# A hybrid decoder layer on one core: its beginning rewritten, and its buffers laid out without gaps

## The chip, the cores and the metric

The kernel runs on one NeuronCore of one Trainium2 chip. The metric is device time in microseconds (us), as the median of several executions. One execution was also recorded by the hardware profiler; the profile and the trace quoted here come from that one. The engines are named as the profile names them: PE (TensorE, matrix products; PEld is its weight load), ACT (ScalarE), DVE (VectorE), POOL (GpSimd) and SP (SyncE, which here only issues transfers). A 128x512 tile means 128 partitions with 512 elements of four bytes each.

## The reference, cut to what matters

For 2048 tokens of width 1024, one layer in float32:

```python
mod = silu(c) @ w_ada + b_ada                       # one row of 3 x 1024
shift, scale, gate = split(mod, 3)
h = rmsnorm(x, g_norm) * (1 + scale) + shift        # rmsnorm over the 1024 columns
proj = h @ w_in                                     # 2832 columns, cut into gq gk gv ga gz sq sk sv sz
z = ga @ w_decay + b_decay
o_gla = rmsnorm_per_head(gla_chunked(gq, gk, gv, log_sigmoid(z) / 16)) * silu(gz)
q, k = rope(sq), rope(sk)
o_swa = sliding_window_sink_attention(q, k, sv, sinks) * silu(sz)
y = concat(o_gla, o_swa) @ w_out
out = rmsnorm(x + gate * y, g_final)
```

The gated linear attention (gla) has 4 heads, worked in two pairs; the sliding-window attention (swa) has 8 query heads on 2 key heads, in blocks of 128 tokens.

## The kernel before, in words

**Precision.** A float32 operand of the large products is split into a high part (rounded to the fast format, F32R) and a low part (what is left), and a product is three fast matmuls: high by high, high by low, low by high (`mm3`). Names ending in h and l are these parts: `hh`, `hl` for the normalised input h, `wh`, `wl` for weights.

**Stages.** Tokens are worked in four groups of 512 (u = 0 to 3). For each group, h lies transposed, with 8 tiles over the 1024 columns (k = 0 to 7, called the eight steps of k), and the projection is done in slots of 256 columns, named by what they give: qk0, gz0, gv0 (272 columns, with the decay inputs), qk1, gz1, gv1, kv, sz0, sq0, sq1, sz1. At the end 16 output tiles (`py`) follow, 128 tokens each.

**The beginning (u = 0).** `silu_rows` spreads silu(c) over all partitions: eight float32 products of s_c by an identity matrix, into two 128x512 PSUM tiles (`pb`). `norm0_start` loads the eight 128x512 tiles of the transposed x, squares each on ACT, and sums over the columns by eight float32 products with a matrix of ones (`ss`); 20 products without use (`warm`, `pw`) follow; two ACT steps make the reciprocal root `rstd`. For each step of k, `ada_load` brings 1 MB of w_ada, `ada_cols` multiplies it by the silu rows on DVE (four 128x512 pieces, whose sums are collected in `part` and added), and ACT makes the shift and the scale of that column tile; `norm0_k` multiplies x by rstd (POOL, or DVE for k = 0), applies scale and shift on ACT, copies the high part on ACT and subtracts for the low part on DVE. Beside it, three 128x256 weight tiles of the slots qk0, gz0 and sz0 are loaded and split (high on ACT, low on POOL). `proj_t_outer` then runs all three slots together, step of k by step of k, 18 matmuls of 512 columns each, into six PSUM tiles (`po`).

**Weights.** In group 0 each slot is loaded raw (`wr`), split, used, and its two parts are written to a buffer in HBM (`wc`); groups 1 to 3 fetch the parts from there (`fetch`). The SBUF tile of a slot is 128 x 8 x 272; a slot of 256 columns leaves 16 columns of each of the 8 rows empty. Two such tiles (one in use, one being filled) are there for each part, and three staging tiles (`st`) for raw weights.

**Keys.** `k_rows` (L993) transposes the rotated keys of a group into one PSUM tile (`pkr`, bank pqk), copies them from there four times on ACT into the key tiles `kst`, and subtracts four times on DVE, reading `pkr` again. The same bank serves the transposed queries (`pq`).

**What sets the order.** All operations are first recorded (`Order`, L85) with a duration from a small cost model. `issue` (L207) then plays them through that model, engine by engine: of the operations that are ready at an engine's next free time, the one with the lowest number goes first (the numbers are lowered by `lift` for urgent and raised by `LATER` for unhurried ones). The resulting sequence of each engine is emitted; on the chip each engine follows its sequence and waits for its operands by semaphores. All large transfers are issued by SP, in order, on one queue. Because every operation is emitted by one helper, most rows of the profile carry the same line, and tiles are told apart by name.

## Time and profile before

| what | value |
|---|---|
| median of 3 runs | 867.58 us (866.02 to 867.92) |
| the profiled execution's own time | 866.11 us |
| its span in the profile | 864.4 us |
| PE busy | 839.3 us, 97% of the span |
| DVE, ACT, POOL busy | 66%, 55%, 43% |
| transfers | 179.90 MB, mean 208 GB/s |

A timeline row reads: start in us, length in us, engine, line, operation, output <- inputs (partitions x elements), count; in square brackets the idle time of the engine just before, and what ended it. A row with x2 or more holds several instructions. A wait list reads: who waited <- for whom: total us, how often, longest. A row of windows reads: from:to, length, then busy us of PE, PEld, DVE, ACT and POOL with their instruction counts, the clock granted to PE (1.00 is full), the mean busy share of the 16 transfer engines and GB/s. PE's busy time includes the modelled end of each matmul, so the distance from one start to the next tells its rate.

### The profile page before, as it was taken

To read this page: it belongs to the slowest core of one execution; us is meant where nothing else is said; L and a number is where in the kernel's file an instruction comes from. 1 tells how busy PE (TensorE), PEld (TensorE's weight loads), DVE (VectorE), ACT (ScalarE), POOL (GpSimd) and SP (SyncE) were. 2 spreads that over 40 slices of the span, in tenths; PEclk is the share of its full clock that TensorE was granted. 3 is DMA by queue.
4 is the path that set the end of the run, shared out by engine and by line. 5 is a ranking of instruction groups with operands and counts; after the bars stand their busy time and mean duration, and the time that the engine had idled before them with its cause. 6 is when DMAs were issued, how large, how long until landed. Compare 5 with 4: busy or idle time off the path is not lost. (4 is left out here: it accounts for less than half of the span.)

```text
span 864.4 us, 14761 instructions
## 1 busy us (share of the span) xinstructions
PE 839.3 (97%) x5126; PEld 730.9 (85%) x5126; DVE 572.9 (66%) x1157; ACT 476.0 (55%) x1197; POOL 372.4 (43%) x437
## 2 busy tenths in 40 slices
...
DMA  8999996963443475755337746669585855444411
GB/s 295 364 364 337 346 311 218 330 222 120 165 165 117 143 229 191 248 172 182 116 124 243 236 155 201 243 214 327 166 288 187 257 171 180 147 139 148 145 70 49
DMA packets 153119, 179.90 MB, mean 208 GB/s; under 512 B 8739, under 2 KB 121430, under 8 KB 151894
## 3 DMA queue, kind: packets, MB, share of 16 engines
...
q10 hardware_dynamic: 864, 0.04, 0.1%
HBM read 134.78 MB, written 44.17 MB: 207 GB/s over the span
## 5 line engine op out<-in xcount | busy, mean ns | idle before, releaser
L420 PE MATMUL py<-woh,m 128*128 128x512 f32 (+2 forms) x528 | 160.6, 385 | 0.0
L420 PEld LDWEIGHTS py<-woh,m 128*128 128x128 f32 x528 | 98.5, 188 | 19.5 <-issue 0.2
L420 PE MATMUL py<-wol,m 128*128 128x512 f32 (+2 forms) x264 | 101.6, 385 | 0.0
L373 POOL TENSOR_TENSOR r<-r,gf 128x512 f32<-128x512 f32 x31 | 45.1, 1453 | 116.4 <-ACT xr L373 116.4
L373 ACT ACTIVATE ge<-ge 128x512 f32<-128x512 f32 x96 | 60.7, 632 | 32.6 <-DVE ge L373 28.7
L420 PE MATMUL pn<-wh_gv,hh 128*128 128x272 f32 (+1 forms) x256 | 73.3, 286 | 0.9 <-DVE rope L373 0.9
L420 PE MATMUL pn<-wl_gv,hh 128*128 128x272 f32 (+1 forms) x256 | 73.5, 287 | 0.0
L420 PE MATMUL pn<-wh_gv,hl 128*128 128x272 f32 (+1 forms) x256 | 73.4, 287 | 0.0
L420 PE MATMUL pn<-wh_sq,hh 128*128 128x256 f32 x256 | 72.5, 283 | 0.0
L420 PE MATMUL pn<-wl_sq,hh 128*128 128x256 f32 x256 | 72.2, 282 | 0.0
L420 PE MATMUL pn<-wh_sq,hl 128*128 128x256 f32 x256 | 72.1, 282 | 0.0
L373 DVE TENSOR_TENSOR r<-py,xr 128x512 f32<-128x512 f32 (+2 forms) x33 | 22.3, 675 | 58.0 <-PE py L420 55.2
L373 ACT ACTIVATE s<-s,nm 128x128 f32<-128x128 f32 x128 | 50.0, 392 | 17.5 <-DVE nm L373 17.3
L420 PEld LDWEIGHTS py<-wol,m 128*128 128x128 f32 x264 | 49.6, 188 | 9.8
L373 POOL TENSOR_TENSOR s<-s,den 128x512 f32<-128x512 f32 x32 | 35.8, 1120 | 50.2 <-DVE den L373 25.1
L373 POOL TENSOR_TENSOR xt<-xt,rstd 128x512 f32<-128x512 f32 x31 | 41.9, 1359 | 27.9 <-ACT rstd L373 16.4
L373 POOL TENSOR_TENSOR o<-o,zs 128x128 f32<-128x128 f32 x64 | 31.3, 509 | 46.3 <-DVE o L373 46.3
L420 PEld LDWEIGHTS pn<-wh_gv,hh 128*128 128x128 f32 x256 | 48.2, 188 | 1.6 <-PE pn L420 1.1
L420 PEld LDWEIGHTS pn<-wl_sq,hh 128*128 128x128 f32 x256 | 48.2, 188 | 0.9 <-issue 0.2
L420 PEld LDWEIGHTS pn<-wh_sq,hh 128*128 128x128 f32 x256 | 48.3, 188 | 0.8 <-issue 0.2
L420 PEld LDWEIGHTS pn<-wh_sq,hl 128*128 128x128 f32 x256 | 48.3, 189 | 0.7
L420 PEld LDWEIGHTS pn<-wl_gv,hh 128*128 128x128 f32 x256 | 48.2, 188 | 0.7
...
## 6 DMA issues: line engine op xcount, KB each, us to landing
...
```

What stands on the lines that cost most here:

```text
L373: return order.add(eng, lambda: real(*args, **kw), dur, ins, outs, lock=lock, nbytes=nbytes)
L420: return od.add("PE", lambda: T.matmul(o, l, r, start=start, stop=stop), dur, [l, r] + ([] if start else [o]), [bank if start and bank is ...
```

## The change

**The beginning.** c is loaded by ACT's queue, so SP starts with x. x comes in four transfers of 128x1024 (rows of 4 KB in memory) instead of eight of 128x512; two column tiles are squared (one on ACT, one on DVE), added on DVE, and summed by one product, so `ss` takes four products instead of eight. The silu rows use F32R parts of s_c and of the identity: 16 fast products into one 128x1024 PSUM tile in a pool of its own. `ada_cols` takes each 128x1024 row of w_ada in one DVE instruction that also gives its sum. The three first weight tiles come as one transfer of 128x768 per step of k, and are split in two pieces. h's high part is written by ACT directly from x (with scale and shift), without a copy; for odd k (`WITH_V`) DVE applies scale and rstd, and makes the low part with the shift. The last step of rstd is written to PSUM, from where DVE reads it for k = 0; ACT copies it to SBUF. For k = 0 the 512 tokens are worked in two halves. 13 products without use stand in place of 20. The table of angles (`rope_tables`) is recorded to start after the last low part of h. sz0 takes the third place in the weight buffer.

**Keys.** `k_rows` copies `pkr` once into an SBUF tile `kt` (in the one buffer `ge`, which the gates and `dgh` use too); ACT and POOL copy from there, and DVE subtracts from there.

**Layout.** A slot of 256 columns lies in its tile without gaps (`flat_w`), so that a whole part is one row of 8 KB. `mixd`, the buffer of the mixed heads, is ordered by token block; xT by token group.

**The planner.** An operation that its model takes to need the port shared by DVE and POOL is ready no earlier than that port's free time (`PATIENCE`), and the model moves transfers at 330 GB/s in its first 20 us. The PSUM tiles ppt and ppo move to a pool `att2` that is opened after the beginning.

Three places show what moves. First, DVE at its start (`sq` are squares of x, `s_c` the silu column, `b` a bias row, `rr` and `rn` the table of angles, `wa` a row of w_ada). Before:

```order
L373 TENSOR_SCALAR s_c<-s_c 128x8
L373 RECIPROCAL s_c<-s_c 128x8
L373 TENSOR_TENSOR s_c<-s_c,c_sb 128x8
L373 TENSOR_SCALAR b_125<-b_sb 128x8
L373 TENSOR_TENSOR b_125<-b_125,g_sb 128x8
L373 CAST pos_f<-pos_i 128x16
L373 TENSOR_TENSOR rr_240<-pos_f,fr 128x512
L373 TENSOR_SCALAR rn_239<-rr_240 128x512
L373 TENSOR_SCALAR rn_239<-rn_239 128x512
L373 SCALAR_TENSOR_TENSOR wa_153,ap_157<-wa_153,pb_104 128x512
```

The same place on DVE in the changed kernel, from its first row:

```order
L377 TENSOR_TENSOR sq_113<-xt_111 128x512
L377 TENSOR_SCALAR s_c<-s_c 128x8
L377 RECIPROCAL s_c<-s_c 128x8
L377 TENSOR_TENSOR s_c<-s_c,c_sb 128x8
L377 TENSOR_TENSOR sq_115<-xt_111 128x512
L377 CAST s_ch<-s_c 128x8
L377 TENSOR_TENSOR sq_112<-sq_112,sq_113 128x512
L377 TENSOR_TENSOR s_cl<-s_c,s_ch 128x8
L377 TENSOR_TENSOR sq_114<-sq_114,sq_115 128x512
L377 TENSOR_TENSOR sq_117<-xt_111 128x512
L377 TENSOR_SCALAR b_123<-b_sb 128x8
L377 TENSOR_TENSOR sq_116<-sq_116,sq_117 128x512
```

The table of angles has gone from here, and four squares and four additions (six of the eight are among these rows) have come in ahead of the first product with w_ada.

Second, SP behind the loads of the beginning (`wr` raw weights, `wc` the buffer of split parts). Before:

```order
L373 DMA wr_sz_205<-in_w_in 128x256
L373 DMA wc<-wh_gz_131 128x512
L373 DMA wc<-wh_gz_132 128x512
L373 DMA wc<-wh_gz_133 128x512
L373 DMA wc<-wl_gz_135 128x512
L373 DMA wc<-wh_qk_129 128x8x256
L373 DMA wc<-wl_qk_130 128x8x256
L373 DMA wr_gv_214<-in_w_in 128x544
```

In the changed kernel:

```order
L377 DMA wr_first_180<-in_w_in 128x768
L377 DMA wr_gv_185<-in_w_in 128x544
L377 DMA wr_gv_186<-in_w_in 128x544
L377 DMA wr_gv_187<-in_w_in 128x544
L377 DMA wc<-wh_first 128x2048
L377 DMA wr_gv_188<-in_w_in 128x544
L377 DMA wc<-wl_first 128x2048
```

The last raw piece of gv0 now has one write of 1 MB between it and the others instead of six writes.

Third, PE at the start of slot sq0 (`pn` products of a slot, `pk`, `pc`, `po` pieces of gla; the digit behind hh or hl is k). Before:

```order
L420 MATMUL pn_321<-wh_sq_300,hh_5_193 128x256
L420 MATMUL pn_321<-wl_sq_301,hh_5_193 128x256
L420 MATMUL pn_321<-wh_sq_300,hl_5_194 128x256
L420 MATMUL pn_321<-wh_sq_300,hh_6_200 128x256
L420 MATMUL pn_321<-wl_sq_301,hh_6_200 128x256
L420 MATMUL po_279<-sT,v 128x128 x4
L420 MATMUL po_278<-qk_229,R_272 128x128
L420 MATMUL po_279<-qk_229,R_272 128x128
```

In the changed kernel:

```order
L424 MATMUL pn_303<-wh_sq_278,hh_0_153 128x256
L424 MATMUL pn_303<-wl_sq_279,hh_0_153 128x256
L424 MATMUL pn_303<-wh_sq_278,hl_0_154 128x256
L424 MATMUL pn_303<-wh_sq_278,hh_1_157 128x256
L424 MATMUL pn_303<-wl_sq_279,hh_1_157 128x256
L424 MATMUL pn_303<-wh_sq_278,hl_1_158 128x256
L424 MATMUL pn_303<-wh_sq_278,hh_2_161 128x256
L424 MATMUL pn_303<-wl_sq_279,hh_2_161 128x256
L424 MATMUL pn_303<-wh_sq_278,hl_2_162 128x256
L424 MATMUL pn_303<-wh_sq_278,hh_3_165 128x256
L424 MATMUL pn_303<-wl_sq_279,hh_3_165 128x256
L424 MATMUL pn_300<-wh_sq_278,hh_6_177 128x256 x2
```

Before, the first product with k = 6 stood directly behind those with k = 5. Now the two token blocks of `pn_300` stop at k = 5, the next block `pn_303` takes eleven products with k = 0 to 3, and only then does k = 6 follow; the pieces of gla `pk`, `pc`, `pu` and the first `po`, which before stood among the products of slot kv, have also come in behind the first product of sq0.

```diff
-WARM = (20, 20)
+WARM = 13
+WITH_V = (1, 3, 5, 7)
...
+PATIENCE = 0.0
...
+            if need[x[2]][2][0].lock:
+                t = max(t, self.port - PATIENCE)
...
-            self.wire = max(self.wire, t + 0.9) + o.bytes / 370e3
+            self.wire = max(self.wire, t + 0.9) + o.bytes / (330e3 if t < 20 else 370e3)
...
-    mixd = dram.tile([P, 8, S], F32, name="mixd")
+    mixd = dram.tile([P, S // P, 8, P], F32, name="mixd")
...
+        i.deps.add(ready[0])
...
+    rows = Pool("rows", 1, PSUM, into=ctx2)
...
-        rows = []
-        for i in range(2):
-            pb = att.tile([P, NB], F32, name=f"pb{i}", tag="ppt" if i == 0 else "ppo")
-            for k in range(4):
-                j = 4 * i + k
-                mmul(pb[:, k * P:(k + 1) * P], s_c[:, j:j + 1].broadcast_to([P, P]), ident, True, True)
-            rows.append(pb)
-        return rows
+        pb = rows.tile([P, D], F32, name="pb")
+        for j in range(KT):
+            with od.together():
+                for i in range(2):
+                    mmul(pb[:, j * P:(j + 1) * P], s_p[i][:, j:j + 1].broadcast_to([P, P]), ident_r,
+                         i == 0, i == 1)
+        return pb
...
-        part = begin.tile([P, 2, 2], F32, name=f"ap{j}", tag="ap", bufs=3)
         for i in range(2):
-            for h in range(2):
-                w_ = wa[:, i, h * NB:(h + 1) * NB]
-                V.scalar_tensor_tensor(w_, w_, 1.0, srow[h], op0=ALU.mult, op1=ALU.mult,
-                                       accum_out=part[:, i, h:h + 1])
-        V.tensor_reduce(ada[:, j], part, AX.X, ALU.add)
+            V.scalar_tensor_tensor(wa[:, i], wa[:, i], 1.0, srow, op0=ALU.mult, op1=ALU.mult,
+                                   accum_out=ada[:, j, i:i + 1])
         A.activation(ashift[:, j:j + 1], ada[:, j, 0:1], AF.Identity, bias=b_sb[:, j, 0:1])
...
+            raws[k] = begin.tile([P, 3, n], F32, name=f"wr_first{k}", tag="st0", bufs=3)
+            SY.dma_start(raws[k].rearrange("p a b -> p (a b)"), src[:, k])
+
+        def part(k):
+            raw = raws.pop(k)
+            both = ([t[:, k] for t in t0], raw[:, 0]), ([t[k] for t in t1], raw[:, 1:3])
+            for d, r in both:
+                (G.tensor_copy if k == 0 else A.copy)(d[0], r)
+            for d, r in both:
+                G.tensor_tensor(d[1], r, f(d[0]), ALU.subtract)
...
+                for k in range(KT):
+                    ops.append(SY.dma_start(f(to[:, :, k]), f(t1[i][k])))
+            od.lift = 0
+            for x in ops:
+                x.deps.add(after)
...
+    def flat_w(t, n):
+        return t.rearrange("p k n -> p (k n)")[:, :t.shape[1] * n].rearrange("p (k n) -> p k n", n=n)
...
+        if copy is None:
+            A.activation(th, xt, AF.Identity, bias=ashift[:, j:j + 1], scale=amul[:, j:j + 1])
         A.activation(xt, xt, AF.Identity, bias=ashift[:, j:j + 1], scale=amul[:, j:j + 1])
-        copy(th, xt)
-        V.tensor_tensor(tl, xt, f(th), ALU.subtract)
+        if copy is not None:
+            copy(th, xt)
...
-            xt = begin.tile([P, NB], F32, name=f"xt0_{j}", tag="xt0", bufs=KT)
-            SY.dma_start(xt, xT[j * P:(j + 1) * P, 0:NB])
-            xt0.append(xt)
-            sq = begin.tile([P, NB], F32, name=f"sq{j}", tag="sq", bufs=3)
-            A.activation(sq, xt, AF.Square)
-            i = mmul(ps, ones, sq, j == 0, j == KT - 1)
-        warm(WARM[1], i)
+        xs = begin.tile([P, KT, NB], F32, name="xt0")
+        for j in range(0, KT, 2):
+            SY.dma_start(xs[:, j:j + 2], xT[:, 0, j:j + 2])
+        for j in range(0, KT, 2):
+            sq = [stp.tile([P, 2, MAXN], F32, name=f"sq{j}", tag="st").rearrange("p a b -> p (a b)")[:, :NB],
+                  stp.tile([P, NB], F32, name=f"sq{j + 1}", tag="xs", bufs=2)]
+            A.activation(sq[0], xs[:, j], AF.Square)
+            V.tensor_tensor(sq[1], xs[:, j + 1], xs[:, j + 1], ALU.mult)
+            V.tensor_tensor(sq[0], sq[0], sq[1], ALU.add)
+            i = mmul(ps, ones, sq[0], j == 0, j == KT - 2)
+            xt0.extend([xs[:, j], xs[:, j + 1]])
+        warm(WARM, i)
         r = begin.tile([P, NB], F32, name="rstd0")
         A.activation(r, ps, AF.Ln, bias=eps_c, scale=1.0 / D)
-        A.activation(r, r, AF.Exp, scale=-0.5)
-        rstd[0] = r
+        A.activation(ps, r, AF.Exp, scale=-0.5)
+        rstd[:] = r, ps
+
+    def norm0_scale(j):
+        if j == 0:
+            V.tensor_tensor(xt0[j], xt0[j], rstd[1], ALU.mult)
+            A.copy(rstd[0], rstd[1])
+        elif j not in WITH_V:
+            G.tensor_tensor(xt0[j], xt0[j], rstd[0], ALU.mult)
 
     def norm0_k(j):
-        xt = xt0[j]
-        (G if j else V).tensor_tensor(xt, xt, rstd[0], ALU.mult)
         hh[j] = hp.tile([P, NB], F32R, name=f"hh0_{j}", tag="hh")
         hl[j] = hp.tile([P, NB], F32R, name=f"hl0_{j}", tag="hl")
-        h_split(j, xt, hh[j], hl[j], A.copy)
+        if j in WITH_V:
+            x_ = xt0[j]
+            V.scalar_tensor_tensor(x_, x_, amul[:, j:j + 1], rstd[0], op0=ALU.mult, op1=ALU.mult)
+            A.activation(hh[j], x_, AF.Identity, bias=ashift[:, j:j + 1])
+            ready[0] = V.scalar_tensor_tensor(hl[j], x_, ashift[:, j:j + 1], f(hh[j]),
+                                              op0=ALU.add, op1=ALU.subtract)
+            return
+        for h in halves(j):
+            h_split(j, xt0[j][:, h], hh[j][:, h], hl[j][:, h], None)
+
+    def halves(j):
...
+            for h in halves(k):
+                for i, w in enumerate(ws):
+                    for ct in range(2):
+                        cs = slice(ct * P, (ct + 1) * P)
+                        p = ps[2 * i + ct]
+
+                        for n, (a, b) in enumerate(((w[0], hh), (w[1], hh), (w[0], hl))):
+                            mmul(p[:, h], a[k][:, cs], b[k][:, h], k == 0 and h.start == 0 and n == 0,
+                                 k == KT - 1 and n == 2, p)
...
+            SY.dma_start(mixd[:, u * TPU:(u + 1) * TPU, 2 * pair + h], rt.rearrange("p (a b) -> p a b", a=TPU))
...
+        kt = near.tile([P, NB], F32, name="kt", tag="ge", bufs=1)
+        A.copy(kt, pt)
         for kv in range(2):
             src = half[kv]
             kh, kl = [x[:, P:] for x in kst[kv]]
-            for h in (src, half[1 - kv]):
-                A.copy(kh[h], pt[src])
-        for kv in range(2):
-            src = half[kv]
-            kh, kl = [x[:, P:] for x in kst[kv]]
+            A.copy(kh[src], kt[src])
+            G.tensor_copy(kh[half[1 - kv]], kt[src])
             for h in half:
-                V.tensor_tensor(kl[h], pt[src], f(kh[src]), ALU.subtract)
+                V.tensor_tensor(kl[h], kt[src], f(kh[src]), ALU.subtract)
 
     def sink_sq(u, kv, qr_of):
...
     def first_k(k):
         ada_load(k)
-        for w in wk:
-            w[2](k)
+        w_load(k)
+        if k == 0:
+            w_part(k)
+            norm0_scale(k)
         ada_cols(k)
         norm0_k(k)
+        if k > 0:
+            w_part(k)
+        if k + 1 < KT:
+            norm0_scale(k + 1)
 
     ps = proj_t_outer(wk, first_k)
     V.tensor_copy(pf, pos_i)
     loader(0, 0)
-    od.lift = LATER
-    for w in wk:
-        w[3]()
-    od.lift = 0
+    w_keep(ready[0])
     ctx2.close()
     keep = Pool("keep", 1)
     tmp = Pool("tmp", 2)
```

115 lines of the change are left out of this document (65 added, 50 removed).

## The prediction

> **What bounds the kernel now.** I read the page first, then the chain of waits, then PE's own waits, and then the timelines of the places that the change touches. The page:
>
> ```profile
> span 864.4 us, 14761 instructions
> PE 839.3 (97%) x5126; PEld 730.9 (85%) x5126; DVE 572.9 (66%) x1157; ACT 476.0 (55%) x1197; POOL 372.4 (43%) x437
> ```
>
> PE is the bound: 97% busy, and the other engines have a third of the time free or more. The chain ends with one unbroken stretch of the output products, of which the change alters nothing:
>
> ```profile
> 706.72 151.03 PE py L420 x684
> ```
>
> So the change can gain only where PE stands still or runs slowly before 706 us. The list of PE's waits names where (us in all, times, longest):
>
> ```profile
> PE pb L420 <- DVE b L373: 3.6, 1, 3.6
> PE pq L425 <- DVE kst L373: 2.9, 3, 1.1
> PE po L420 <- ACT hh L373: 2.8, 1, 2.8
> PE ppo L420 <- POOL ph L373: 2.2, 2, 1.3
> ...
> PE pg L420 <- ACT ga L373: 0.2, 1, 0.2
> ```
>
> The first and third lie in the beginning, the second in the keys; all fifteen rows sum to 17.9 us. The timeline of the beginning shows the chain behind them:
>
> ```profile
> 1.25 5.21 SPq L373 DMA_DIRECT2D xt<-in_xT  x8
> 3.57 3.75 PE L420 MATMUL pb<-ident,s_c 128*128 128x128 f32 x16 [3.57 <-DVE b L373]
> 4.69 1.30 ACT L373 ACTIVATE sq<-xt 128x512 f32<-128x512 f32 x2 [1.91 <-DMA xt<-in_xT]
> 7.11 7.97 PE L420 MATMUL ss<-sq,ones_r 128*128 128x512 f32 x16
> 12.56 0.69 DVE L373 SCALAR_TENSOR_TENSOR wa<-wa,pb 128x512 f32<-128x512 f32 x1 [3.71 <-PE ss L420]
> 14.92 4.63 PE L420 MATMUL pw<-ident,ones_r 128*128 128x128 f32 x40
> 15.18 0.69 ACT L373 ACTIVATE rstd<-ss,eps_c 128x512 f32<-128x512 f32 x1
> 16.90 0.62 ACT L373 ACTIVATE rstd<-rstd 128x512 f32<-128x512 f32 x1
> 17.60 1.60 POOL L373 TENSOR_TENSOR xt<-xt,rstd 128x512 f32<-128x512 f32 x1 [0.41 <-ACT rstd L373]
> 17.99 1.75 DVE L373 TENSOR_TENSOR xt<-xt,rstd 128x512 f32<-128x512 f32 x1
> 19.84 0.41 ACT L373 CAST wh_qk<-wr_qk 128x256 fp32r<-128x256 f32 x1 [2.04 <-DMA wr_qk<-in_w_in]
> 20.87 0.81 ACT L373 ACTIVATE xt<-xt,ashift,amul 128x512 f32<-128x512 f32 x1
> 21.71 0.62 ACT L373 CAST hh<-xt 128x512 fp32r<-128x512 f32 x1
> 22.38 1.22 PE L420 MATMUL po<-hh,wh_qk 128*128 128x512 f32 x2 [2.83 <-ACT hh L373]
> 28.11 0.63 PE L420 MATMUL po<-hh,wh_qk 128*128 128x512 f32 x2
> 57.03 0.28 PE L420 MATMUL pn<-wh_gv,hh 128*128 128x272 f32 x1
> ```
>
> The useful products begin at 22.38 (k = 0) and 28.11 (k = 1). From there to the first product of gv0 at 57.03, seven steps of k take 4.13 us each. That is PE's own pace, 18 matmuls of 0.23 each (4.13 / 18), so a gain at the start of k = 1 is kept to 57 us if the transfers and splits keep up. Step k = 0 takes 5.73 us instead of 4.13: its 1.6 us too much is the clock, granted at half behind the wait of 2.83 (the columns after the length are busy us of PE, PEld, DVE, ACT and POOL, then the clock, the share of the transfer engines and GB/s):
>
> ```profile
> 2.00:10.00 8.00, 6.43 (x22) 4.87 (x23) 2.51 (x9) 2.80 (x6) 0.11 (x1) 1.00 0.89 265
> 10.00:22.00 12.00, 9.55 (x52) 6.40 (x50) 8.48 (x20) 7.24 (x16) 5.84 (x7) 1.00 1.02 365
> 23.00:24.00 1.00, 1.00 (x4) 0.81 (x3) 1.00 (x1) 0.57 (x2) 0.73 (x2) 0.50 1.17 440
> 40.00:60.00 20.00, 20.00 (x100) 16.94 (x99) 18.19 (x39) 14.54 (x31) 8.76 (x12) 1.00 1.04 373
> 60.00:80.00 20.00, 18.51 (x114) 16.06 (x113) 12.71 (x21) 15.70 (x34) 1.30 (x1) 1.00 0.96 322
> 80.00:100.00 20.00, 20.00 (x169) 18.70 (x168) 13.62 (x29) 11.85 (x27) 5.89 (x8) 1.00 1.05 363
> ```
>
> The same rows show a second limit close by: until 100 us the transfer engines are full nearly all the time.
>
> **The beginning, step by step.** x is issued at 0.80 instead of 1.25. The first 256 KB landed 3.44 us after their issue (4.69 against 1.25), of which 1 us is the bytes at 265 GB/s. Pairs of 512 KB then land at about 4.8, 6.4, 8.0 and 9.6 at 330 GB/s, a value I take between the 265 and 365 of the windows. The last pair is squared (0.65), then added (0.69 for a 128x512 of two operands): 11.0. PE is later than that. Eight `ss` products took 7.97, one about 1.0; the first, on the cold clock, runs until 9.6, the sixteen `pb` products until 11.4, and three more `ss` until 14.0. The fast `pb` are not in the trace; a full-speed matmul of 128 columns is bounded by the 4.63 / 40 = 0.12 of `pw`, a slow one by 3.75 / 16 = 0.23, so 1.9 to 3.7, and I take 1.9, since PE is already warm behind the first `ss`. Then the two steps of rstd (0.69 and 0.62), with amul between them as before: 15.9. DVE multiplies from PSUM in about 0.69, what its 128x512 operations with one SBUF operand take, instead of 1.75 beside POOL: 16.6. ACT's first half with its start: 17.2, and PE begins at 17.3. The three casts of weights that held ACT from 19.84 (0.41 each) until x was scaled at 20.87 are on POOL for k = 0. `pw` fills PE's gap, so k = 0 runs at full clock, 36 half products of 0.12 in 4.3 us, and k = 1 starts at 21.6. The low end is the cold clock lasting until 15.5, which gives 23.1. The high end is x landing at 365 GB/s with everything behind it following, 20.5. **The beginning gives 28.11 - 21.6 = 6.5 us (4.9 to 7.6).**
>
> For the idle gap and the clock, the Trainium skill, TensorE: Matmul & The Clock Gate, Part 1: The HAM clock gate, says that PE starts at half clock, is raised after about 3.4 us of sustained work and falls after an idle window of about that length. The trace fell already behind 2.83 us; by the page alone k = 0 would not have lost its 1.6 us, and what the beginning gives would be 4.9; the row decides.
>
> For the multiplication from PSUM, the Trainium skill, SBUF — State Buffer, Who interferes with whom, says that a DVE operation with two SBUF operands and a POOL operation on SBUF exclude one another, and one with at most one SBUF operand does not wait. The rows 1.75 and 1.60, which overlap, agree. By that rule the changed subtractions of the keys, too, come under this lock (the second rival).
>
> The remaining work of u = 0 moves little. ada_cols reads the same 128x1024 twice per k in two instructions instead of four, without the reduction: DVE does less. Halves of 256 columns double the instructions of k = 0 but not their columns; I charge 0.3 us for the extra starts (none at best, 0.6 at worst, one 0.03 per product for 18). The last raw piece of gv0 stands behind a write of 1 MB that itself waits for the last cast, so I charge 0.3 (0 to 0.7). The table of angles moves behind u = 0's low parts: into the stretch from 60 to 80 us, where DVE is busy 12.71 of 20 us, so 0; without that free time the rotation of the first queries would wait for it.
>
> **The transfers behind it.** PE arrives 6.5 us earlier at slot sq0, whose raw weights come late in SP's queue. Before:
>
> ```profile
> 90.10 0.37 SPq L373 DMA_DIRECT2D wr_sq<-in_w_in  x1
> 93.97 0.61 ACT L373 CAST wh_sq<-wr_sq 128x512 fp32r<-128x512 f32 x1
> 98.38 0.28 PE L420 MATMUL pn<-wh_sq,hh 128*128 128x256 f32 x1
> ```
>
> The first product came at 98.38, so at about 91.9 now. Adding up the sizes of SP's transfers, 31.45 MB lay up to the end of the last raw piece of sq0, which was in place by 93.97; now it is 32.2 MB, and at the rates of the windows 17.8 of them are left at 42 us. At 353 GB/s (the mean of the rows from 40 to 100) they end at 92.4; with a latency of 2.5 (3.44 less 1.0, above) the piece is there at 94.9 and split at 96.2 (0.61 on ACT, 0.69 on DVE). PE needs it at 91.9 + 7.6 = 99.5, since the new order puts some 45 products of 256 columns (0.115 each, half of 0.23) and some 40 pieces of gla of 128 (0.06) between the first product and k = 6. So it fits, by 3 us. At 322 GB/s for all of it the piece is split at 101.1 and PE stands 1.6; sq1 and sz1 follow on the same queue, and I double it for them, 3.2. I charge 0.5.
>
> **The keys.** PE's transposes of queries wait for the bank of `pkr`:
>
> ```profile
> 381.60 0.60 PE L425 MATMUL pkr<-ident,kr 128*128 128x128 f32 x4
> 382.24 1.78 ACT L373 CAST kst<-pkr 64x512 fp32r<-64x512 f32 x3 [0.24 <-PE pkr L425]
> 385.38 2.10 DVE L373 TENSOR_TENSOR kst<-pkr,kst 64x512 fp32r<-64x512 f32 x3 [0.65 <-ACT kst L373]
> 387.62 0.41 PE L425 MATMUL pq<-ident,qr 128*128 128x128 f32 x2 [0.86 <-DVE kst L373]
> L373 DVE TENSOR_TENSOR kst<-pkr,kst x16: 674/689/695, 117.7 to 553.3; 64x512 fp32r<-64x512 f32 x16
> L373 DVE TENSOR_TENSOR hl<-xt,hh x8: 692/813/1833, 22.4 to 50.2; 128x512 fp32r<-128x512 f32 x8
> ```
>
> The bank is held from 381.60 to the last subtraction at 387.48, 5.9 us, by four ACT copies and four DVE subtractions. With one copy into `kt` it is free after about 1.3 us (0.6 on PE, 0.6 on ACT), far before the next `pq`. I count 2.7 of the 2.9 us back (2.3 if the waiting copy stands behind other ACT work). The copies and subtractions then run from SBUF; their readers are score products later in the slot. If that cover went, the extra copy (0.6) and a locked subtraction (1.83 at worst against 0.69, as `hl<-xt,hh` shows) would count.
>
> **Layout and the rest of the order.** Long rows for weights: group 0 moved 373 GB/s with rows of 1 to 2 KB, so longer rows are counted as nothing, with the chance of a gain only in the first 10 us, used above. `mixd` is written by gla in rows of 512 B, and read in rows of 4 KB; the transfers behind 100 us have room, as the page's slices of 21.6 us show (tenths of the transfer engines' time):
>
> ```profile
> DMA  8999996963443475755337746669585855444411
> ```
>
> From the seventh slice on, they are mostly half busy. The planner reorders everything behind the beginning. PE's hidden waits before 706 us are at most 18 us (the whole list sums to 17.9), and a new order redistributes those that are neither beginning nor keys, some 8.6 us (17.9 - 3.6 - 2.9 - 2.8). I charge 0.5, with 2.5 to either side, somewhat under a third of it.
>
> **Sum:** -6.5 + 0.3 + 0.3 + 0.5 - 2.7 + 0.5 = -7.6 us. The profiled execution's own time is 866.11, 1.5 below the median of the runs shown; it becomes 858.5, and the median of 867.58 becomes **860.0 us**. Its own range, with the ends of the terms not all at once, is 857 to 864.
>
> **Rivals.** First, the transfers bind in group 0: they move 322 GB/s, as from 60 to 80 us, and the slots wait 3.2 us instead of 0.5, which gives 860.0 + 2.7 = 862.7. For it speaks a share of 0.96 to 1.05 in these rows; against it, that 322 fell in a stretch in which PE itself waited (18.51 of 20 busy) and SP was held by late parts.
>
> Second, the lock: the subtractions of the keys now have two SBUF operands and POOL, which gets copies of its own, delays them and other work so far that the 2.7 us come back at the scores: 860.0 + 2.7 + 0.7 = 863.4. For it speak the 1.75 and 1.83; against it, that POOL is busy 43%.
>
> Third, slower than before: the raw weights of group 0 run at the 265 GB/s of the first window, instead of at 353, because the new pattern (3 KB and 2 KB rows read, 8 KB rows written between them) holds the queue. From 42 us 17.8 MB take 67.2 us, the last piece of sq0 is split at 113.0, PE needs it at 99.5, and the wait of 13.5 takes the place of everything gained: 860.0 - 0.5 + 13.5 = 873.0. It decides from about 288 GB/s downwards, where the wait reaches 8.1 us. Against it: the long windows from 10 to 100 us show 322 to 373.
>
> Fourth, that the new order removes a part of the 8.6 us of other hidden waits, 4 of them: 856.
>
> **How the numbers follow.** The forecast has 0.50, the transfers 0.19, the lock 0.10, the slower case 0.10, the better order 0.11. The range 855.5 to 867.0 holds the forecast and the first two rivals with their own spread and more than half of the fourth; it leaves out the third. A measurement of this kernel can tell 0.2%, 1.7 us, from no change. Faster by that means below 865.8. It gets 0.50 + 0.11 and nearly all of the first two rivals, less what adds up to a loss: 0.83. Within 0.2%, where the transfers cost 6 us and more, 0.07. Slower, the third rival, 0.10.
>
> **What would show it.** Right: the first `po` at 17 to 18 us with the clock at 1.00, k = 1 at 20.5 to 23.2, gv0 at 50 to 52, no wait of `pq` for `kst`, first sq0 product at 91 to 93 with a wait below 1 us for `wh_sq`. Wrong: the clock below 1.00 behind `pw`; steps of k longer than 4.13 with waits for `hh` or `wl`; PE waiting for `wh_sq` or `wl_gv` by several us; key subtractions near 1.8 us; or gv0 at 50.5 and a sum of PE's waits behind it several us above the present one.

## The result, and the profile after

| | before | changed |
|---|---|---|
| median of the runs (4 each, same chip) | 866.80 us (865.08 to 867.92) | 875.41 us (872.50 to 875.87) |
| the profiled execution's span | 864.4 us | 870.8 us |
| ratio to before, 95% interval | | 1.0094 (1.0065 to 1.0123) |

The change makes the kernel slower by 0.94%, about 8 us. The forecast was 860.0, with a range of 855.5 to 867.0. The profiled execution of the changed kernel is the fastest of its four (872.50 us), so the two profiles, of one execution each, show only 6.4 us of the difference. The page of the changed kernel:

```profile
span 870.8 us, 14663 instructions
PE 841.4 (97%) x5122; PEld 732.0 (84%) x5122; DVE 578.7 (66%) x1132; ACT 470.8 (54%) x1178; POOL 374.6 (43%) x436
DMA packets 76000, 179.90 MB, mean 207 GB/s; under 512 B 8420, under 2 KB 24855, under 8 KB 72727
```

The other engines have as much free time as before, and the same bytes now go in half as many packets (before: 153119). Still PE ends later. Its waits sum to 22.3 us in 16 rows, before to 17.9 in 15. That alone does not place the loss, because 4.0 of these 4.4 us stand in the first row, ahead of a beginning that now has less to do behind it. The first rows of the list, and one further on:

```profile
PE ss L424 <- DVE s_cl L377: 7.6, 1, 7.6
PE pq L429 <- DVE qs L377: 2.9, 2, 2.1
PE pk L429 <- DVE qk L377: 2.8, 1, 2.8
...
PE pq L429 <- ACT kt L377: 0.6, 1, 0.6
```

PE's first product now waits 7.6 us, where before it waited 3.6. The row of `pq` for `kst` (2.9 before) is gone, and rows of `pq` for `qs` (2.9) and for `kt` (0.6) and of `pk` for `qk` (2.8, before 0.5) have come.

The difference over the program, read from the two traces at the moment when PE has worked the same share of the columns of its useful products, so without `pb`, `ss` and `pw` (after minus before, us; the place by the time it has in the kernel before; where the two orders differ, an entry is good to about 1 us):

| place before | 25 | 29 | 57 (gv0) | 86 | 107 | 128 | 193 | 360 | 591 | 613 | 655 | end |
|---|---|---|---|---|---|---|---|---|---|---|---|---|
| after - before | -2.2 | -0.9 | -0.4 | -1.6 | -1.9 | +3.0 | +2.8 | +5.9 | +4.9 | +8.4 | +7.7 | +6.5 |

So the beginning gives 0.4 us at gv0 and not 6.5, and 4.9 us are lost in one piece between 107 and 128 us. Of the later losses, the clearest is that of 3.5 us between 591 and 613; elsewhere the difference moves by up to 3 us either way. The beginning first, in the timeline of the changed kernel:

```profile
4.94 0.21 ACT L377 ACTIVATE s_c<-c_sb 128x8 f32<-128x8 f32 x1 [2.42 <-DMA c_sb<-in_c_cols]
7.57 2.05 PE L424 MATMUL ss<-sq,ones_r 128*128 128x512 f32 x2 [7.57 <-DVE s_cl L377]
9.52 0.42 PE L424 MATMUL pb<-ident_r,s_cl 128*128 128x128 f32 x1
12.51 0.41 PE L424 MATMUL pb<-ident_r,s_cl 128*128 128x128 f32 x1
12.73 5.13 PE L424 MATMUL ss<-sq,ones_r 128*128 128x512 f32 x6
17.70 3.06 PE L424 MATMUL pw<-ident,ones_r 128*128 128x128 f32 x26
19.44 0.69 DVE L377 TENSOR_TENSOR xt<-xt,ss 128x512 f32<-128x512 f32 x1 [4.03 <-ACT ss L377]
21.39 0.35 PE L424 MATMUL po<-hh,wh_first 128*128 128x256 f32 x1 [0.63 <-ACT hh L377]
27.11 0.50 PE L424 MATMUL po<-hh,wh_first 128*128 128x512 f32 x1 [1.18 <-ACT hh L377]
56.62 0.28 PE L424 MATMUL pn<-wh_gv,hh 128*128 128x272 f32 x1
92.99 0.40 PE L424 MATMUL pn<-wh_sq,hh 128*128 128x256 f32 x2
```

c, now on ACT's queue, is there at 4.94, so PE starts at 7.57. The timeline of the kernel before has these two rows to compare, for c and, further on, for a tiny operation that comes up below:

```profile
2.57 0.21 ACT L373 ACTIVATE s_c<-c_sb 128x8 f32<-128x8 f32 x1 [0.49 <-DMA c_sb<-in_c_cols]
104.34 0.17 DVE L373 TENSOR_TENSOR nwt<-nwt,ss 128x4 f32<-128x4 f32 x1
```

The sixteen fast `pb` follow one another at 0.21 us (14 steps from 9.52 to 12.51), and the three `ss` behind them take 5.13, 1.7 each, where before eight took 7.97. The first `pw` (0.118 each) are the first products at full rate, ten microseconds after PE's start. The trace's record of the clock begins just there, at 17.43 us (before: at 8.50), and the clock column shows 1.00 where there is no record; for this stretch the rate is read from the distance of the starts. `po` begins 1.0 us earlier than before, and so does k = 1 (27.11 against 28.11). Of that 0.4 us is left at gv0 (56.62 against 57.03): step k = 1 takes 4.89 us instead of 4.13, and in it PE waits for a low part of h (`PE po L424 <- DVE hl L377: 0.4, 1, 0.4`). Three of the runs below, those with the writes early, with `qs` first and with the gate later, leave this beginning as it is; in their traces `po` came at 20.10 to 20.99 and gv0 at 55.31 to 56.24. So the execution shown is the latest of four, and the beginning gives 0.4 to 1.7 us.

Then the keys of group 0, first PE and then DVE and POOL in the timeline:

```profile
111.93 0.60 PE L429 MATMUL pkr<-ident,kr 128*128 128x128 f32 x4
114.57 0.41 PE L429 MATMUL pq<-ident,qr 128*128 128x128 f32 x2 [0.65 <-ACT kt L377]
121.91 0.41 PE L429 MATMUL pq<-ident,qr 128*128 128x128 f32 x2 [2.15 <-DVE qs L377]
115.36 1.21 DVE L377 TENSOR_TENSOR nwt<-nwt,ss 128x4 f32<-128x4 f32 x1
118.77 2.11 DVE L377 TENSOR_TENSOR kst<-kt,kst 64x512 fp32r<-64x512 f32 x3
120.91 0.86 DVE L377 TENSOR_TENSOR qs<-pq,qs 64x256 fp32r<-64x256 f32 x2
115.26 1.30 POOL L377 TENSOR_TENSOR v<-v,zs 128x512 f32<-128x512 f32 x1
```

`pq` is put directly behind the keys and waits 0.65 for the copy `kt`. The next `pq` waits 2.15, since the subtraction `qs` that frees its bank stands on DVE behind the subtractions of the keys and behind tiny operations that have become long: `nwt` of 128x4 takes 1.21 instead of 0.17 and ends together with POOL's `v` (116.57 and 116.56). The windows of the changed kernel show that the clock then falls (by the trace's record it is 0.50 for 3.4 us, from 123.25 to 126.66), and, in the last row, the same pattern at the late place (columns as before: us; busy of PE, PEld, DVE, ACT, POOL; clock; share; GB/s):

```profile
117.00:122.00 5.00, 2.85 (x14) 2.07 (x13) 4.87 (x10) 1.73 (x3) 1.68 (x2) 1.00 0.91 331
122.00:125.00 3.00, 3.00 (x11) 2.42 (x12) 2.91 (x7) 1.36 (x3) 0.00 (x0) 0.71 0.71 205
125.00:128.00 3.00, 3.00 (x19) 2.85 (x18) 1.62 (x8) 1.38 (x4) 1.10 (x4) 0.72 1.02 376
600.00:610.00 10.00, 7.04 (x49) 6.66 (x48) 8.09 (x14) 5.33 (x10) 1.74 (x2) 0.90 0.93 350
```

The waits of 0.65 and 2.15 and the half clock (1.7 us lost in 3.4) account for 4.5 of the 4.9 us lost there. At the late place one wait of PE stands ahead of the same fall of the clock (0.50 from 607.94 to 611.35):

```profile
607.71 0.88 PE L429 MATMUL pk<-ident,qk 128*128 128x128 f32 x4 [2.80 <-DVE qk L377]
```

Before, the row of this late stretch read 9.83 busy at full clock:

```profile
600.00:610.00 10.00, 9.83 (x80) 9.49 (x79) 8.14 (x14) 3.23 (x7) 4.89 (x6) 1.00 0.66 227
```

### The profile page after: what moved, and what is told of

It reads as the page before. It is cut to its first block, busy times and chain, and to the rows that moved or that the text cites. A ratio compares the mean times of both kernels' runs of the same rounds, so it can differ in the third digit from the quotient of the medians.

```text
span 870.8 us, 14663 instructions
## 1 busy us (share of the span) xinstructions
PE 841.4 (97%) x5122; PEld 732.0 (84%) x5122; DVE 578.7 (66%) x1132; ACT 470.8 (54%) x1178; POOL 374.6 (43%) x436
## 2 busy tenths in 40 slices
DMA packets 76000, 179.90 MB, mean 207 GB/s; under 512 B 8420, under 2 KB 24855, under 8 KB 72727
## 5 line engine op out<-in xcount | busy, mean ns | idle before, releaser
L424 PE MATMUL py<-woh,m 128*128 128x512 f32 (+2 forms) x528 | 160.7, 385 | 0.1
L424 PEld LDWEIGHTS py<-woh,m 128*128 128x128 f32 x528 | 98.4, 188 | 20.1 <-DVE r L377 0.5
L424 PE MATMUL py<-wol,m 128*128 128x512 f32 (+2 forms) x264 | 101.4, 384 | 0.0
L377 POOL TENSOR_TENSOR r<-r,gf 128x512 f32<-128x512 f32 x31 | 45.8, 1480 | 114.6 <-ACT xr L377 111.9
L377 ACT ACTIVATE ge<-ge 128x512 f32<-128x512 f32 x96 | 60.6, 631 | 37.4 <-DVE ge L377 36.2
L424 PE MATMUL pn<-wh_gv,hh 128*128 128x272 f32 (+1 forms) x256 | 73.7, 288 | 0.0
L424 PE MATMUL pn<-wl_sq,hh 128*128 128x256 f32 x256 | 73.5, 288 | 0.2 <-DMA wl_sq<-wc 0.2
L424 PE MATMUL pn<-wh_sq,hl 128*128 128x256 f32 x256 | 73.4, 287 | 0.0
L424 PE MATMUL pn<-wh_gv,hl 128*128 128x272 f32 (+1 forms) x256 | 73.3, 287 | 0.0
L424 PE MATMUL pn<-wl_gv,hh 128*128 128x272 f32 (+1 forms) x256 | 73.3, 287 | 0.0
L424 PE MATMUL pn<-wh_sq,hh 128*128 128x256 f32 x256 | 72.7, 286 | 0.0
L377 DVE TENSOR_TENSOR r<-py,xr 128x512 f32<-128x512 f32 (+2 forms) x33 | 22.3, 675 | 62.5 <-PE py L424 62.5
L377 ACT ACTIVATE s<-s,nm 128x128 f32<-128x128 f32 x128 | 50.1, 393 | 20.7 <-DVE nm L377 20.5
L424 PEld LDWEIGHTS py<-wol,m 128*128 128x128 f32 x264 | 49.6, 188 | 9.7
L377 POOL TENSOR_TENSOR s<-s,den 128x512 f32<-128x512 f32 x32 | 35.6, 1111 | 43.7 <-DVE den L377 31.8
L377 POOL TENSOR_TENSOR xt<-xt,rstd 128x512 f32<-128x512 f32 x27 | 38.0, 1411 | 37.2 <-ACT rstd L377 15.6
L424 PEld LDWEIGHTS pn<-wl_sq,hh 128*128 128x128 f32 x256 | 49.4, 193 | 1.5 <-DMA wl_sq<-wc 0.4
L377 POOL TENSOR_TENSOR qr<-qr,rope 128x256 f32<-128x256 f32 x32 | 27.0, 863 | 54.1 <-DVE rope L377 54.1
L424 PEld LDWEIGHTS pn<-wh_sq,hl 128*128 128x128 f32 x256 | 49.3, 193 | 1.0 <-issue 0.3
L424 PEld LDWEIGHTS pn<-wh_sq,hh 128*128 128x128 f32 x256 | 49.2, 193 | 0.8 <-issue 0.2
L424 PEld LDWEIGHTS pn<-wh_gv,hh 128*128 128x128 f32 x256 | 48.4, 189 | 0.6
L424 PEld LDWEIGHTS pn<-wl_gv,hh 128*128 128x128 f32 x256 | 48.4, 189 | 0.5
```

The lines of the kernel that those rows point to most:

```text
L377: return order.add(eng, lambda: real(*args, **kw), dur, ins, outs, lock=lock, nbytes=nbytes)
L424: return od.add("PE", lambda: T.matmul(o, l, r, start=start, stop=stop), dur, [l, r] + ([] if start else [o]), [bank if start and bank is ...
```

## The experiments

Two ways of editing are used. In some runs the sequence of every engine stays as it is and one thing is moved or replaced in it by hand; in the others the planner draws the order anew after the edit. Each run is compared with the kernel before on the same chip; the ratio is the run's time to that kernel's, with its 95% interval. The timelines and waits of a run are those of its one profiled execution.

### The beginning, in the changed kernel's own order

The first run loads c first on SP, and puts the silu steps ahead of the squares on DVE and `pb` ahead of `ss` on PE. The second only makes the rows by eight float32 products again. The third does both.

```diff
-    A.dma_start(c_sb, c_cols)
+    nc.sync.dma_start(c_sb, c_cols)            # first of SP; s_c ahead of sq, pb ahead of ss
```
```diff
-        mmul(pb[:, j * P:(j + 1) * P], s_p[i][:, j:j + 1].broadcast_to([P, P]), ident_r, i == 0, i == 1)
+        T.matmul(pb[:, j * P:(j + 1) * P], s_c[:, j:j + 1].broadcast_to([P, P]), ident, start=True, stop=True)
```

> The changed kernel with c on SP's queue ahead of x, the silu operations on DVE ahead of the squares, and the row products on PE ahead of ss; every other instruction stays in the changed kernel's order. Theory A (late c): in the changed kernel PE began at 7.57 only because s_c came 2.4 us later and behind squares. Then pb begins at about 3.9, the clock rises some 5 us later, ss ends near 12 and the first po comes at 15.5 to 16 instead of 21.39; the total falls by about 5 us. Theory B (the fast row products leave the clock low): pb begins at 3.9 all the same, but ss still runs at half rate until about 12.5, ends at 13 to 14, and the first po comes at about 17.2.

> The changed kernel with the silu rows by eight float32 products as before, in the changed kernel's order. Theory A: PE still begins at 7.57, so the first po moves by at most 0.5 us (about 21). Theory B: the clock rises about 5 us after 7.57, so the last three ss take 0.86 each instead of 1.66, ss ends near 16 instead of 17.86 and the first po comes at about 19.5.

> Both edits together. Theory A: the same as with c early alone, 15.5 to 16. Theory B: pb from 3.7 to 7.4, ss at full rate behind the additions on DVE, end near 12.2, first po at about 15.7 where c early alone gives 17.2; total 5 to 6 us below the changed kernel.

Measured: c early 873.49 us, ratio 1.0080 (1.0056 to 1.0104); float32 rows 872.24, 1.0053 (1.0028 to 1.0079); both 871.51, 1.0055 (1.0031 to 1.0079). All three intervals overlap that of the changed kernel (1.0065 to 1.0123), and the 5 us and more that were expected of the first and the third are not there. The timeline of PE with the float32 rows alone:

```profile
7.52 2.04 PE L444 MATMUL ss<-sq,ones_r 128*128 128x512 f32 x2 [7.52 <-DVE s_cl L397]
9.35 3.56 PE L557 MATMUL pb<-ident,s_c 128*128 128x128 f32 x16
12.75 2.74 PE L444 MATMUL ss<-sq,ones_r 128*128 128x512 f32 x6
19.03 0.36 PE L444 MATMUL po<-hh,wh_first 128*128 128x256 f32 x1 [0.63 <-ACT hh L397]
```

The same three `ss` at the same moment (12.75, against 12.73) take 2.74 us instead of 5.13, and `po` comes 2.4 us earlier. The rows themselves are no dearer: a float32 product counts as two here, and 16 of them take 3.56 us, where the 16 fast ones took 4.1 (8.63 to 12.73). With c early and fast rows, the `ss` stay slow, though PE has worked since 3.69:

```profile
7.99 6.74 PE L445 MATMUL ss<-sq,ones_r 128*128 128x512 f32 x8 [0.65 <-DVE sq L398]
14.57 3.06 PE L445 MATMUL pw<-ident,ones_r 128*128 128x128 f32 x26
```

So PE's late start is not what keeps it slow; with c early and with c late, the fast rows come with the slow `ss`. The clock records begin accordingly: at 17.43 us in the changed kernel, 14.18 with c early, 12.73 with float32 rows and 7.55 with both. But float32 rows are not enough. The run with all moves, further on, has them and an early c; there PE waited 1.54 us behind the rows, the clock record begins at 12.78, and the `ss` are slow again:

```profile
8.73 5.68 PE L457 MATMUL ss<-sq,ones_r 128*128 128x512 f32 x8 [1.54 <-DVE sq L410]
```

What raises the clock is therefore not settled. With both edits the forecast's beginning comes about as far as the first product, and no further. PE and DVE in the timeline of that run:

```profile
16.52 0.36 PE L445 MATMUL po<-hh,wh_first 128*128 128x256 f32 x1 [1.17 <-ACT hh L398]
25.21 0.50 PE L445 MATMUL po<-hh,wh_first 128*128 128x512 f32 x1 [1.47 <-ACT hh L398]
17.45 1.22 DVE L398 SCALAR_TENSOR_TENSOR wa<-wa,pb 128x1024 f32<-128x1024 f32 x1 [2.20 <-DMA wa<-in_w_ada]
20.28 2.44 DVE L398 TENSOR_TENSOR hl<-xt,hh 128x256 fp32r<-128x256 f32 x2
22.64 1.76 DVE L398 SCALAR_TENSOR_TENSOR xt<-xt,amul,rstd 128x512 f32<-128x512 f32 x1
```

`po` starts at 16.52, but w_ada for k = 1 is there only at 17.45, and behind it DVE needs 2.44 us for the low parts of k = 0 and 1.76 for the scaling of k = 1. k = 1 starts at 25.21. Of the 5.9 us at the first `po`, 2.9 are left there and 2.3 at gv0; by the end all of it is gone (+7.4 us, changed +6.5).

### The losses between 107 and 128 us and near 600 us

The next runs keep the changed order but for one move. The first puts 3 MB of the writes that follow the first stage (`w_keep`) into the 8 us in which SP is idle from 39.7 to 47.9 us, so that they don't meet group 0's transfers. The second puts the first four subtractions of the keys on DVE behind the first two `qs`. The third puts two pieces of the output gate, which wait for w_gate, behind the `qk` that PE waits for at the late place. The fourth makes all these moves but the writes, together with c early and the float32 rows.

```diff
-DVE: kst, kst, kst, kst, qs, qs
+DVE: qs, qs, kst, kst, kst, kst
```

> The changed kernel with twelve writes of split parts (k = 0 to 5 of gz0 and sz0, 3 MB) moved on SP ahead of the first 1 MB write, into the 8 us in which SP stands still behind it; all else in the changed kernel's order. Theory C (the loss between 107 and 128 us comes from 3 MB that the transfers fall behind between 40 and 60 us): the raw pieces of sq1 and sz1 come 5 us or more earlier, PE's wait of 2.1 us for qs and the low clock behind it go, total 870 to 871. Theory D (the loss comes from the order on DVE alone, small operations and splits ahead of the qs subtraction): the waits for qs stay within 0.5 us and the total stays at 874 to 876.

> The changed kernel with one thing moved: on DVE the first four subtractions of the keys (kst, group 0) come behind the first two subtractions of the queries (qs) instead of ahead of them. Theory E (the early free bank lets PE start pq early, and its wait only moved from kst to qs, 2.15 us, and takes the clock down to 0.7 for some 6 us behind it): the second pq no longer waits at 119 us, the clock stays at 1.00 from 122 to 128, and what stands behind 130 us comes 3 to 4 us earlier; total about 871.5. Theory C' (late raw weights): DVE is late anyway, the wait returns at the scores or the next pq, gain below 1 us.

> The changed kernel with one thing moved: on DVE two of the eight steps of the second output gate (gate<-wg) come behind the product qk that PE's transposes pk wait for near 605 us, instead of ahead of it. Theory F (the late loss of some 4 us is the new order on DVE): PE's wait of 2.8 us for qk falls to below 0.8, the clock stays at 1.00 there, total 3 to 4 us lower, about 871.5. Rival: qk waits for its own inputs, and the wait stays above 2 us.

> c early, float32 silu rows, the queries' subtractions first and the gate steps later, all at once. If the four causes are separate, the gains add up: 1.2 to 2 from the beginning, 3 to 4 and 3 to 4: about 867, equal to the kernel before. If the late loss is the arrival of w_gate rather than the order, 870.

Measured: writes early 876.00, 1.0089 (1.0057 to 1.0121), with the loss between 107 and 128 as large as before (from -2.4 to +2.7). The writes went where they should, and 383 GB/s moved from 40 to 60 us instead of 223; but the raw pieces of sz1 and sq1 were issued only 0.5 us earlier (95.31 and 105.52 against 95.78 and 106.00). So these 3 MB are neither what the raw pieces wait for nor the cause of the loss; why sz1's are issued 5 us later than in the kernel before (90.70) was not followed. `qs` first 873.74, 1.0081 (1.0054 to 1.0109), from two executions: in its profile the second `pq` waits 1.36 instead of 2.15, the clock does not fall there, and the loss there shrinks from 4.9 to 3.0, but the difference is given back further on. Gate later 873.41, 1.0061 (1.0040 to 1.0081): the wait of `pk` only went from 2.8 to 2.1, so the gate was a small part of it. All moves 869.44, 1.0038 (1.0023 to 1.0053): the best of the changed orders, and still slower than before. In its profile, which is of the fastest of its ten executions, the clock does not fall before 862 us. Mending places one by one recovers part of the loss, and new waits open elsewhere.

### Single parts of the change in the kernel before

Keys as in the changed kernel (the planner draws the order with its old rules); the layout alone (`flat_w`, and `mixd` by token block), where the order is the same as before; both together; and, the other way round, the changed kernel with the old layout.

```diff
+        kt = near.tile([P, NB], F32, name="kt", tag="ge", bufs=1)
+        A.copy(kt, pt)
-            for h in (src, half[1 - kv]):
-                A.copy(kh[h], pt[src])
+            A.copy(kh[src], kt[src])
+            G.tensor_copy(kh[half[1 - kv]], kt[src])
```
```diff
-    mixd = dram.tile([P, 8, S], F32, name="mixd")
+    mixd = dram.tile([P, S // P, 8, P], F32, name="mixd")
-            tiles = [[wp.tile([P, KT, MAXN], ...)]
+            tiles = [[flat_w(wp.tile([P, KT, MAXN], ...), n)]
```

> The kernel before with the new k_rows alone. As predicted (the bank is free early and nothing takes its place): PE's waits of pq for kst, 2.9 us, go, total about 865. Theory E: the waits come back at qs or kt, the sum of PE's waits for these does not fall by more than 1 us, and the total is within 2 us of before or above.

> The kernel before with the new layout alone (weight tiles and staging tiles without gaps, mixd by token block); the order on every engine is that of the kernel before. As predicted: no change, within 0.2% of before (865 to 868.5). Theory I (rows of 512 B written to mixd, or 8 KB rows, hold up the queue): 2 us or more slower. Rival: long rows free transfer time where PE waits for weights, 1 to 2 us faster.

> The kernel before with layout and keys, planned as the keys alone were. If the parts are separate: 4.7 (layout) and 1.3 (keys) less, about 861. If the layout's gain and the keys' are the same waits: 863.

> The changed kernel with the old layout of the weight tiles, the staging tiles and mixd, in the changed kernel's own order. If the layout is worth the same there: 3 to 5 us slower than the changed kernel, 878 to 880. If the layout is what costs in the changed kernel: 872 or below.

Measured: keys 865.09, ratio 0.9986 (0.9968 to 1.0003); layout 863.17, 0.9936 (0.9912 to 0.9959); both 860.18 (857.16 to 860.84), 0.9915 (0.9886 to 0.9945); the changed kernel with the old layout 876.27, 1.0114 (1.0083 to 1.0145).

With the keys alone no wait of `pq` for `kst` is left, and its timeline is 3.5 us ahead at 591 us. All of that is gone by 655: new waits stand there (`pms` for `osq` 1.8, `ppt` for `s` 1.1, `pk` for `qk` 1.0), and with the first the clock falls to 0.50 for 3.4 us (from 637.55). A wait removed in the middle is not a wait removed from the end.

The layout is the surprise, since no change was expected of it. The page of the kernel before with it has

```profile
DMA packets 76831, 179.90 MB, mean 209 GB/s; under 512 B 8739, under 2 KB 24150, under 8 KB 73558
```

and its window at one place of the same order (first this, then that of the kernel before):

```profile
130.00:140.00 10.00, 10.00 (x86) 10.00 (x85) 8.28 (x19) 6.30 (x19) 6.19 (x7) 1.00 0.87 321
```

```profile
130.00:140.00 10.00, 9.05 (x77) 8.88 (x76) 6.84 (x13) 6.03 (x19) 4.80 (x4) 1.00 0.77 245
```

From 130 to 140 us 321 GB/s move instead of 245, and PE is busy 10.00 instead of 9.05. In its timeline the kernel is level with the one before at 128 us (0.4 ahead) and 2.7 us ahead at 193, and it keeps that (2.9 at the end). Why transfers of the same bytes end a wait of PE for DVE's `rope` there was not followed further, and the weight tiles and `mixd` were not tried apart. In the changed kernel no gain of the layout is shown: 1.0114 without it against 1.0094 with it, with intervals that overlap.

Layout and keys together give 6.8 us at the median: 860.18 against 866.94 of the kernel before, about the sum of the two alone (4.7 and 1.3). So this kernel is faster than the kernel before and than the changed one. That 860 is also the forecast's figure is chance: the forecast counted nothing for the layout and 6.5 us for a new beginning, and this kernel has the old beginning and the old planner.

### The beginning and all parts, in the old order

The kernel before, its order kept, with x in pairs, half as many `ss`, rstd in PSUM, h's high part straight from x, and 14 products without use; first alone, then with layout and keys (the order then being that of the run with both). The rows stay float32; the halves and the joint first weights are not in.

```diff
+            if j % 2 == 0:
+                o.fn = lambda j=j: nc.sync.dma_start(xs[:, j:j + 2], xT[:, 0, j:j + 2])
+            else:
+                o.skip = True
+                i.fn = lambda a=even, j=j: T.matmul(ps, ones, a, start=j == 1, stop=j == KT - 1)
```

> The kernel before with a mended beginning, everything behind the beginning in the old order: x in four long transfers, half the squares and the additions on DVE, four ss, rstd read from PSUM for k = 0, hh straight from x, 14 products without use, the table of angles and the first weights of k = 1 behind k = 0's own work; c stays on SP, the silu rows stay float32. Theory (as predicted, with the two faults of the changed kernel mended): first po at 16 to 17 with the clock at 1.00, k = 1 not before about 24 because w_ada for k = 1 lands near 17.5, gv0 at 53 to 54; total 3 to 4 us below before if nothing takes it back later, 865 if it is taken back.

> Layout, keys and the mended beginning on the kernel before, in the order that the kernel before with the keys has. Theory H (the parts are worth what they show alone, and the new order of the changed kernel costs the rest): 4.7 + 1.3 + 3, about 858. Rival (the parts get in each other's way, the transfers bind in the first group): 862 or above.

Measured: 865.48, 0.9982 (0.9961 to 1.0004), and 859.97 (858.65 to 861.48), 0.9916 (0.9886 to 0.9946). The timeline of the first:

```profile
18.35 0.72 PE L454 MATMUL po<-hh,wh_qk 128*128 128x512 f32 x2 [2.37 <-ACT hh L701]
28.19 0.74 PE L454 MATMUL po<-hh,wh_qk 128*128 128x512 f32 x2 [3.66 <-ACT hh L701]
```

k = 0 starts 4.0 us earlier than before (22.38), and k = 1 waits 3.66 us and starts where it did (28.11). By the trace's record the clock is at 0.50 behind both waits (19.4 to 22.9 and 29.7 to 33.1 us), and gv0 comes at 58.98, 2.0 us later than before, where 53 to 54 was expected; by the end that is made up. A faster first step gains nothing as long as the inputs of k = 1 come when they do, and on top of layout and keys the beginning adds nothing that can be told (859.97 against 860.18). With these parts in the old order the kernel takes 860; the changed kernel, in the order that its planner draws, takes 875.

### The order itself

The planner's port rule alone in the kernel before; the changed kernel with the rule off; the same with c on SP and the float32 rows; the other new rule (330 GB/s in the model's first 20 us) alone in the kernel before; and a change of the model that means nothing, again in the kernel before.

```diff
+            if need[x[2]][2][0].lock:
+                t = max(t, self.port)
```
```diff
-PATIENCE = 0.0
+PATIENCE = 1e9
```
```diff
-            self.wire = max(self.wire, t + 0.9) + o.bytes / 370e3
+            self.wire = max(self.wire, t + 0.9) + o.bytes / (330e3 if t < 20 else 370e3)
```
```diff
-        lap = {"V": 0.076, "A": 0.094, "G": 0.041}.get(e, 0.0)
+        lap = {"V": 0.076, "A": 0.114, "G": 0.041}.get(e, 0.0)
```

> The kernel before with the planner's new rule for operations that need the shared port, and nothing else: only the order changes. Theory G (the new rule costs what is lost behind 105 us): 4 us or more slower than before, 870 or above. Theory H (any new order moves a few waits either way): within 3 us of before, in either direction.

> The changed kernel without the planner's new rule; its beginning and keys as changed. Theory G: 4 us or more faster than the changed kernel, 871 or below. Theory H: 872 to 878; a wait of pq for qs is again found within the first group, since the early free bank is still there.

> The changed kernel with c on SP's queue first, the silu column ahead of the squares on DVE, float32 silu rows, and without the planner's new rule; planned anew. Theory G: beginning 2.3 us better than before and the loss behind 105 us gone, 864 to 866. Theory H: 867 to 873.

> The kernel before, with only the second rule of the new planner: the model moves transfers at 330 GB/s in its first 20 us. Nothing that is computed changes, and the order is drawn anew (1862 lines of PE's order differ). Theory R, that the order before is a favourable draw and nearly any new draw costs several us: 870 to 877. Theory P, that it is the port rule that costs the time: 864.5 to 869, within 0.3% of the kernel before.

> The kernel before, with one number of the model changed by a little and for no reason: the overlap of two ACT operations, 0.094 to 0.114 us. Only the order is drawn anew (3073 lines of PE's order differ). Theory R: 870 to 877, as with the port rule (877.23 against 867.9). Theory P: 864.5 to 869.

| run | median, us | ratio (95%) |
|---|---|---|
| port rule alone | 877.23 | 1.0110 (1.0083 to 1.0139) |
| changed, rule off | 879.45 | 1.0129 (1.0097 to 1.0162) |
| the same, c and rows mended | 875.85 | 1.0088 (1.0055 to 1.0120) |
| transfer rule alone | 864.89 | 0.9957 (0.9937 to 0.9977) |
| neutral new draw | 874.60 | 1.0076 (1.0051 to 1.0101) |

In the first, fourth and fifth, not one operation differs from the kernel before; only their order does. They come out 9.5 us slower, 3.7 us faster and 6.6 us slower (ratio less 1, times 866.8 to 868.1). The neutral draw alone refutes that only the port rule can cost this much, and the transfer rule refutes that every new draw loses. Taking the rule out of the changed kernel does not help either (two executions each). So the changed kernel's order is one draw of many, and these three draws alone scatter over more than 10 us. That its own order is what costs it the time is what is left over, and not shown: no run has exactly its operations in the old order, and sz0's third place in the weight buffer and the pool `att2` were not tried alone. Where the neutral draw loses, its windows show at once (here beside those of the kernel before, second fence):

```profile
620.00:640.00 20.00, 17.35 (x100) 13.39 (x99) 13.45 (x25) 9.30 (x16) 2.05 (x2) 1.00 0.54 179
680.00:700.00 20.00, 16.74 (x91) 12.38 (x91) 15.40 (x26) 10.17 (x20) 13.60 (x15) 0.91 0.37 112
```

```profile
620.00:640.00 20.00, 20.00 (x104) 15.92 (x101) 14.84 (x27) 12.51 (x23) 2.34 (x2) 1.00 0.68 224
680.00:700.00 20.00, 19.48 (x128) 15.98 (x127) 14.53 (x28) 11.46 (x23) 7.74 (x9) 1.00 0.54 161
```

Its timeline is 1.9 us ahead at 613 us and 7.9 behind at 697. In the second window PE waits four times for POOL's `pp`, `ph` and `s` (0.25 to 1.07 each) and once for `qk` (0.41), and behind them the clock is at 0.50 for 3.4 us, from 693.0 (0.91 in the mean of the window). Each wait is small, and the clock adds to them.

## Why the prediction was wrong, step by step

**What bounds the kernel.** Right: PE, 97% busy, and the time is decided by where it stands or runs slowly before the output products. The last stretch of these was untouched, as stated.

**The beginning, -6.5 (4.9 to 7.6).** Wrong: -1.0 at the start of k = 1, and -0.4 at gv0. c was not costed at all, and its load on ACT's queue came 2.4 us later (4.94 against 2.57); but the sum does not fail there, for it has the first `ss` run until 9.6, and the second `pb` did start at 9.52. It fails at the next two terms. The fast `pb` were taken at 1.9, "since PE is already warm behind the first `ss`"; they were over at 12.7 instead of 11.4. PE was not at full rate for another five microseconds, so the three `ss` ended at 17.7 instead of 14.0. The range's "cold clock lasting until 15.5" was too short. The second error is behind this one: in the changed kernel PE waited 1.18 us for `hh` of k = 1, and the run with early c and float32 rows shows it whole. With `po` at 16.52, earlier than forecast, k = 1 still came at 25.21, because w_ada of k = 1 landed at 17.4 and the low parts and scaling on DVE took 2.44 and 1.76. The working gave k = 1 the end of k = 0 (21.6) and never asked when its own inputs come. What was right in it: DVE's multiplication from PSUM took 0.69, and behind `pw` at 0.118 the clock stayed full through k = 0 of the changed kernel.

The Trainium skill, SBUF — State Buffer, Who interferes with whom, on which that multiplication was weighed, lets an operation with at most one SBUF operand pass beside POOL. The 0.69 at 19.44 does not test that, since POOL stood still from 16.67 to 20.83; but in the run with the beginning in the old order the same multiplication took 0.69 at 16.70 while POOL's `xt` ran (16.75, 1.27 us), which agrees. The Trainium skill, TensorE: Matmul & The Clock Gate, Part 1: The HAM clock gate, has the clock raised after about 3.4 us of sustained work. That does not fit the fast rows: 10.1 us passed from PE's start (7.57) to the first products at full rate (17.70), and, with c early, 10.9 (3.69 to 14.57).

**Halves, gv0's last raw piece, the angles, +0.6 together.** The size was about right, for another reason: 0.6 us of the gain of k = 1 are gone at gv0, but they go in step k = 1 (4.89 us, with the wait of 0.4 for `hl`), which the forecast had named as a sign of being wrong. Behind the last `po` (56.39) gv0 follows at 56.62 without a wait, and by 107 us the kernel is 1.9 ahead. The forecast's gv0 at 50 to 52 fell with the beginning.

**The transfers, +0.5, and the slower rival.** The mechanism did not happen: PE's list has no row for `wh_sq`. sq0's first product came at 92.99, in the forecast's 91 to 93, but that is luck: PE was only 0.4 us ahead at gv0, and the new order has moved pieces of gla behind this product. The last raw piece of sq0 was split at 104.2 instead of 96.2, and was in time all the same, since PE came to it later as well. The windows of the changed kernel (the first row shows the clock column for the slow `ss`):

```profile
10.00:22.00 12.00, 11.37 (x51) 8.36 (x51) 5.88 (x12) 3.87 (x9) 4.06 (x5) 1.00 0.98 400
40.00:60.00 20.00, 20.00 (x101) 16.93 (x100) 18.94 (x31) 13.03 (x28) 7.15 (x9) 1.00 0.63 223
60.00:80.00 20.00, 19.59 (x120) 17.36 (x119) 17.84 (x28) 14.21 (x29) 3.01 (x3) 1.00 0.99 350
80.00:100.00 20.00, 19.78 (x175) 18.92 (x174) 13.96 (x31) 14.57 (x32) 7.06 (x8) 1.00 1.01 376
```

From 40 to 100 they move 316 GB/s in the mean, above the 288 below which the rival was to decide; the 223 of the first stretch show in no wait of PE. The rival had the right sign for a wrong reason.

**The keys, -2.7.** The wait for `kst` did go, as the working says; "the bank is free early, far before the next `pq`" held in the kernel before with the keys alone. But that alone gained only 1.2 us at the end, and its interval does not exclude no change. In the changed order `pq` came directly behind the keys and waited for the copy (0.65), then for `qs` behind the subtractions (2.15), and the clock fell. The wait moved to the next operation in DVE's sequence. The lock rival saw a part of it. The subtractions of the keys in the changed kernel (shortest, median and longest in ns):

```profile
L377 DVE TENSOR_TENSOR kst<-kt,kst x16: 676/690/1198, 117.6 to 548.8; 64x512 fp32r<-64x512 f32 x16
```

Most lie at 0.69, a few reach 1.20; but a tiny operation beside POOL took 1.21.

**The layout, counted as nothing.** Wrong by about 5 us in the good direction: alone it gave 4.7 us at the median, and 5.5 by the ratio (0.9936). The argument was that group 0 already moves 373 GB/s; the gain is not there but from 130 us on, where the working had written "the transfers have room".

**The rest of the order, +0.5 with 2.5 to either side.** This is the step that failed most, and the one that turned the sign. It bounded the effect of a new order by the waits that the old one has: 8.6 us, a third of it either way. That bounds what a new order can win. It says nothing of what it can lose, since waits that the old order does not have are in no row of its profile. Three orders of the same operations came out at -3.7, +6.6 and +9.5 us. The forecast's figure was met by chance, 859.97 and 860.18, by kernels that have the layout and the keys without the new planner. Against these the changed kernel's 875.4 is about 15 us more, and its beginning, which is ahead by 0.4 at gv0 and 1.9 at 107 us, does not explain that. That a new order can cost this much is shown; that it costs all of it here is argued.

**Chances.** Faster got 0.83, slower 0.10. With draws that scatter by several microseconds to both sides and a sum of -7.6, of which 6.5 hung on one chain, slower should have had a third.

**Open.** What makes one draw good and another bad was not found: the losses are many waits of 0.3 to 2.8 us at places that differ from draw to draw (107 to 130, 590 to 613, 620 to 700 us), with the clock at half behind some of them. Why the layout's gain shows only from 130 us on, and less of it in the changed order, is open too.
